# A two-block transformer on one Trainium2 core: attention matmuls moved to full-array float32r on stacked hi and lo parts

## The chip, the cores and the metric

The kernel runs on one core of a Trainium2 chip. The time is the device time of one execution in microseconds (us), and smaller is better. Before the change the median of three runs is 3154.35 us (3149.34 to 3155.27).

## What is computed

Two hybrid layers and two further layers (called even and odd here) act on 512 tokens of width 1024; all tensors are float32. Cut to the parts that matter, a hybrid layer is

```python
proj = rms_norm(x) @ w_in                      # nine pieces of 256 columns
ret  = bidirectional_retention(rq, rk, rv)     # 4 heads of 64, scores times a decay, no softmax
pool = multiscale_pool(pv)
na   = neighbourhood_attention(nq, nk, nv)     # 4 heads of 64, 256 keys for each block of 128 queries
mo   = memory_attention(mq, mk, mv)            # 4 heads of 64, 256 memory keys
x    = x + (sum of sigmoid(h @ w_gate) * (branch @ w_branch)) @ w_out
x    = x + ffn(x)                              # hidden width 2816
```

The even layer has sliding window attention (8 heads of 64, window 128) and latent attention (8 heads whose keys have 64 plain and 32 rotary channels, the rotary ones shared by all heads). The odd layer has 16 heads of 64 with a causal mask and dilated patterns. Each of the two is followed by cross attention (4 heads of 128) and an FFN.

## The kernel before

**Projections.** Activations lie feature-major, as 8 tiles of 128 channels by 512 tokens, each split into a part `hh` rounded to float32r and the rest `hl`. A weight chunk is loaded by SP (`ws`), rounded by ScalarE (`wh`, line 209) and its rest is taken by VectorE (`wl`, line 210). `mm3` (lines 217 to 219) then issues three float32r matmuls, hi·hi, lo·hi and hi·lo; `proj_tok` (lines 252 to 254) does the same with 256 moving columns. These are about 12,600 of the 15,023 TensorE instructions.

**Scores.** For two heads of 64, `stack_q` makes a tile for each head with the hi part of the query on one half of the partitions and the lo part on the other. `stack_k` gives the hi part of a head's key on both halves, and one tile `k[2]` with the lo parts of both heads. `scores` then needs two float32r matmuls, one of 128 rows (line 400) and one of 64 rows (line 401):

```python
nc.tensor.matmul(out=out, lhsT=q[b][:, qs], rhs=ks(k[b]), start=True, stop=False)
nc.tensor.matmul(out=out, lhsT=q[b][p, qs], rhs=ks(k[2])[p], start=False, stop=True)
```

Retention does the same with keys and queries exchanged (lines 714 and 715). The latent heads take one plain float32 matmul over 96 rows (line 1076).

**Weighted sums.** After the softmax (lines 425 to 440, mostly VectorE) the probabilities of a query block are transposed by TensorE (line 448), copied to SBUF as float32 (`PT`, line 451) and multiplied with the values in float32. The two heads go to the two halves of one PSUM tile `O`, each with 64 columns of the array: lines 471 (causal), 782 (neighbourhood), 494 (memory), 1029 (sliding window). Retention multiplies the scores with the decay on VectorE (line 717) and goes straight on (line 721, 512 moving columns).

**Order.** A scheduler fixes the order of each engine's instructions when the kernel is built. The code gives it the order of priority: `ORDER` for the hybrid layer (`R` retention, `N` neighbourhood, `M` memory, `B` the gated branches), and in `even` and `odd` the projection of the next heads ahead of the attention of these. `chunk` raises the priority of weight loading. Activations share one pool of 25 buffers (`act`, tag `a`); PSUM has two buffers each for `acc`, `S` (scores), `T` (transposes) and `O`.

Of the kernel before, what the change touches and what calls it, by code (L numbers as in the profile page):

```python
# [9 lines left out]
F32 = mybir.dt.float32  # L10
# [8 lines left out]
S = 512  # L19
# [79 lines left out]
class Net:  # L99
    def __init__(self, ctx, tc, a):  # L100
# [7 lines left out]
        self.pp = en(name="pp", bufs=4)  # L108
# [37 lines left out]
    def gains(self, *which):  # L146
        """Gain vectors as columns: rows of 128 are loaded and transposed on TensorE."""
# [31 lines left out]
    def split(self, src, scale=None, hi=None, lo=None):  # L179
        """hi/lo fp32r pair of src * scale."""  # L180
# [14 lines left out]
    def chunk(self, src, kt, n):  # L195
        """src: list of (dram ap [kt*128 rows, cols], column offset)."""
# [24 lines left out]
    def proj(self, hs, W, c0, ncols, evac, n=512, tags=("acc",)):  # L221
        """Feature-major W[:, c0:c0+ncols]^T @ h; evac(tile index, psum)."""
# [17 lines left out]
    def proj_tok(self, hs, ws, n, toks, evac, tags=("acc",)):  # L240
        """Token-major h^T W for chunks ws (list of (hi, lo, kt)); evac(token tile index, psum [128, n])."""
# [24 lines left out]
    def rsqrt(self, src, w, scale, out=None, last=False):  # L266
        """(src * scale + EPS) ** -0.5 for a small tile."""
# [16 lines left out]
    def norm_stats(self, acc, dim, name, want_bc=True):  # L284
        """acc: [128, 512] sums of squares over channel tiles -> token-major rstd [128, 4] and its broadcast."""
# [15 lines left out]
    def prep(self, k, g, start=False):  # L301
        """Split g * x for the next layer and add up its squares."""
# [45 lines left out]
    def feature_major(self, tiles, c):  # L348
        """Channels 128 c ... of token-major tiles [128, 2, *] -> PSUM [128, tokens]."""
# [10 lines left out]
    def stack_q(self, src, view=lambda t: t, gp=False):  # L360
        """Two heads of 64 on the partitions of src -> for each head a tile with its hi and its lo part."""
# [11 lines left out]
    def stack_k(self, src, g=None, gp=False, out=None):  # L373
        """Two heads of 64 on the partitions of src -> for each head its hi part twice, and the lo parts of both."""
        nc = self.nc
        out = out or [self.stack_tile(src.shape[-1], gp) for _ in range(3)]
# [9 lines left out]
        kl = out[2]  # L386
        for b in range(2):
            p = slice(64 * b, 64 * b + 64)
            if g is None:
                nc.vector.tensor_tensor(out=kl[p], in0=src[p], in1=out[b][p].bitcast(F32), op=OP.subtract)  # L390
            else:
                nc.vector.scalar_tensor_tensor(out=kl[p], in0=src[p], scalar=g[p], in1=out[b][p].bitcast(F32),
# [896 lines left out]
```

## Time and profile before

| what | value |
|---|---|
| median of three runs | 3154.35 us |
| profiled execution, span | 3152.4 us |
| TensorE busy | 3083.4 us, 98% |
| VectorE busy | 1689.0 us, 54% |
| ScalarE busy | 1254.3 us, 40% |
| GpSimd busy | 354.9 us, 11% |
| mean granted TensorE clock | 0.984 |

The page of the profile gives only the span of the profiled execution, which is 2 us under the median. Busy time of TensorE counts a matmul up to its modelled end, so neighbouring matmuls overlap: its real cost is the distance from one start to the next, which the timeline shows. DMA engines are busy 30% of the span.

### The profile page before, as it was taken

The numbers are of one execution on the slowest core, as the hardware profiler recorded it, in microseconds if no ns is written. First come the engines' busy times: TensorE is split into PE (matmuls) and PEld (weight loads), VectorE is DVE, ScalarE is ACT, GpSimd is POOL, SyncE is SP. The second block draws the span as 40 slices with busy tenths as digits, with TensorE's granted clock in tenths as the row PEclk, the third lists the DMA queues.
The fourth block names the chain that finished last, engine by engine and source line by source line (L and its number), as shares of the span: only waits on it lengthen the run. The fifth ranks groups of instructions, "written<-read, shape, count | busy, mean of one in ns | idle before, by whom it ended". The sixth has DMA issues, their size and how long they took to land.

```text
span 3152.4 us, 39048 instructions
## 1 busy us (share of the span) xinstructions
PE 3083.4 (98%) x15023; PEld 2500.8 (79%) x15023; DVE 1689.0 (54%) x3054; ACT 1254.3 (40%) x2126; POOL 354.9 (11%) x635
## 2 busy tenths in 40 slices
PE   7989999999999999999999999999999999999998
PEld 6767788888886778888888668788888777888887
DVE  6555555444565564664445775554446666554444
ACT  6443333222463433432223655432225666442222
POOL 2410121000132011120000101010000000010100
PEclk9989999999999999999999899999999999999999
DMA  5312242233342223332322213233332211333332
GB/s 160 108 46 87 73 134 94 96 98 95 126 126 63 70 84 94 124 98 94 100 91 82 52 38 98 74 100 101 94 97 92 66 57 57 94 92 96 100 95 80
DMA packets 288532, 285.62 MB, mean 91 GB/s; under 512 B 23637, under 2 KB 280026, under 8 KB 288346
## 3 DMA queue, kind: packets, MB, share of 16 engines
q1 hardware_dynamic: 288345, 283.13, 29.4%
q8 instruction: 118, 1.93, 0.3%
q14 instruction: 69, 0.56, 0.1%
HBM read 275.37 MB, written 7.71 MB: 90 GB/s over the span
## 4 chain that ended last, share of the span: by engine, by line
PE 95%; DVE 3%; ACT 1%; DMA 1%; issue 1%; POOL 0%; SPq 0%; DVEq 0%; ACTq 0%
PE p_acc L217 11%; PE p_acc L218 11%; PE p_acc L219 11%; PE p_O L217 7%; PE p_O L218 7%; PE p_O L219 7%; PE p_S L218 7%; PE p_S L217 7%; PE p_S L219 7%; PE p_acc L252 2%; PE p_acc L253 2%; PE p_acc L254 2%; PE p_T L448 2%; PE p_S L401 2%; PE p_O L471 1%; PE p_S L400 1%
## 5 line engine op out<-in xcount | busy, mean ns | idle before, releaser
L210 DVE TENSOR_TENSOR wl<-ws,wh 128x1024 fp32r<-128x1024 f32 (+1 forms) x512 | 613.4, 1198 | 751.7 <-ACT wh L209 750.6
L209 ACT CAST wh<-ws 128x1024 fp32r<-128x1024 f32 (+1 forms) x512 | 516.5, 1009 | 1120.2 <-issue 363.1
L217 PE MATMUL p_acc<-hh,wh 128*128 128x512 f32 x1000 | 394.6, 396 | 1.7 <-DVE x L829 1.7
L218 PE MATMUL p_acc<-hh,wl 128*128 128x512 f32 x1000 | 392.5, 393 | 0.0
L219 PE MATMUL p_acc<-hl,wh 128*128 128x512 f32 x1000 | 391.4, 393 | 0.0
L217 PE MATMUL p_O<-hh,wh 128*128 128x512 f32 x680 | 264.4, 390 | 0.3 <-DVE al L188 0.3
L218 PE MATMUL p_O<-hh,wl 128*128 128x512 f32 x680 | 264.5, 390 | 0.0
L219 PE MATMUL p_O<-hl,wh 128*128 128x512 f32 x680 | 264.4, 389 | 0.0
L218 PE MATMUL p_S<-hh,wl 128*128 128x512 f32 x624 | 244.1, 391 | 2.8 <-DVE wl L210 2.8
L217 PE MATMUL p_S<-hh,wh 128*128 128x512 f32 x624 | 243.7, 392 | 2.5 <-ACT wh L209 2.1
L219 PE MATMUL p_S<-hl,wh 128*128 128x512 f32 x624 | 243.7, 391 | 0.0
L571 POOL TENSOR_TENSOR fa<-fa,R_x 128x512 f32<-128x512 f32 x88 | 115.7, 1317 | 1092.6 <-DVE fa L570 1086.2
L217 PEld LDWEIGHTS p_acc<-hh,wh 128*128 128x128 f32 x1000 | 189.0, 189 | 43.9 <-DVE x L829 2.3
L219 PEld LDWEIGHTS p_acc<-hl,wh 128*128 128x128 f32 x1000 | 188.9, 189 | 40.5 <-issue 0.8
L218 PEld LDWEIGHTS p_acc<-hh,wl 128*128 128x128 f32 x1000 | 189.0, 189 | 39.2 <-issue 1.0
L217 PE MATMUL p_acc<-ah,wh 128*128 128x512 f32 x444 | 177.9, 402 | 1.7 <-DVE mlak L1051 1.7
L218 PE MATMUL p_acc<-ah,wl 128*128 128x512 f32 x444 | 174.0, 392 | 0.0
L219 PE MATMUL p_acc<-al,wh 128*128 128x512 f32 x444 | 172.7, 393 | 0.0
L217 PE MATMUL p_S<-ah,wh 128*128 128x512 f32 x392 | 153.3, 392 | 0.3 <-ACT ah L187 0.3
L218 PE MATMUL p_S<-ah,wl 128*128 128x512 f32 x392 | 153.1, 391 | 0.0
L219 PE MATMUL p_S<-al,wh 128*128 128x512 f32 x392 | 151.7, 389 | 0.0
L217 PEld LDWEIGHTS p_O<-hh,wh 128*128 128x128 f32 x680 | 127.5, 188 | 27.2 <-DVE al L188 0.7
(374 smaller groups left out, 5736.0 us busy)
## 6 DMA issues: line engine op xcount, KB each, us to landing
ws<-w_ffn_in SPq DMA_DIRECT2D x88, 512.0 KB
ws<-w_gate SPq DMA_DIRECT2D x64, 512.0 KB
ws<-l_w_gate SPq DMA_DIRECT2D x44, 512.0 KB
ws<-l_w_up SPq DMA_DIRECT2D x44, 512.0 KB
ws<-w_ffn_out SPq DMA_DIRECT2D x40, 512.0 KB
ws<-l_w_down SPq DMA_DIRECT2D x40, 512.0 KB
ws<-w_in SPq DMA_DIRECT2D x36, 512.0 KB
ws<-l_w_qkv SPq DMA_DIRECT2D x24, 512.0 KB
```

The source lines that it names most:

```text
L209: nc.scalar.copy(wh, st)
L210: nc.vector.tensor_tensor(out=wl, in0=st, in1=wh.bitcast(F32), op=OP.subtract)
L217: nc.tensor.matmul(out=out, lhsT=wh[part, k, cols], rhs=hh[part, hn], start=start, stop=False)
L218: nc.tensor.matmul(out=out, lhsT=wl[part, k, cols], rhs=hh[part, hn], start=False, stop=False)
L219: nc.tensor.matmul(out=out, lhsT=wh[part, k, cols], rhs=hl[part, hn], start=False, stop=stop)
L252: nc.tensor.matmul(out=o, lhsT=hh[:, t0:t0 + 128], rhs=wh[:, kk, :], start=k == 0, stop=False)
L253: nc.tensor.matmul(out=o, lhsT=hh[:, t0:t0 + 128], rhs=wl[:, kk, :], start=False, stop=False)
L254: nc.tensor.matmul(out=o, lhsT=hl[:, t0:t0 + 128], rhs=wh[:, kk, :], start=False, stop=k == K - 1)
L400: nc.tensor.matmul(out=out, lhsT=q[b][:, qs], rhs=ks(k[b]), start=True, stop=False)
L401: nc.tensor.matmul(out=out, lhsT=q[b][p, qs], rhs=ks(k[2])[p], start=False, stop=True)
L448: nc.tensor.transpose(pt[:, 128 * i:128 * i + 128], b, self.ident)
L571: nc.gpsimd.tensor_tensor(out=a, in0=a, in1=R, op=OP.mult)
```

## The change

All matmuls of retention, neighbourhood, memory, sliding window, latent and causal attention become float32r over the full 128 by 128 array.

- `stack_k` makes four tiles, the lo part of each head now on both halves as well, so that both matmuls of `scores` have 128 rows.
- Values are kept as `[hi | lo]` side by side, 128 columns (`stack_v`, a ScalarE and a VectorE operation). `transposes` leaves the transposed probabilities as a hi and a lo tile, and `weigh` issues two matmuls for each head.
- The result stands in one PSUM tile for each head, its two halves still to be added: `join` copies one half (ScalarE) and adds the other (VectorE).
- `attend_causal` handles two query blocks at a time, so most products have 256 moving columns; a block on the diagonal and all of neighbourhood attention have 128. Sliding window attention puts both heads side by side in the moving operand.
- A latent head takes three float32r matmuls, with the shared rotary key stacked once (`krot`).
- Neighbourhood attention loads its value tiles for each pair of heads (64 small DMAs in a layer where there were 32).
- `P` and `PT` move to the pool of the stage, with 4 or 5 and 5 or 6 buffers; cross attention keeps float32 (`split=False`).

```diff
     def stack_k(self, src, g=None, gp=False, out=None):
-        out = out or [self.stack_tile(src.shape[-1], gp) for _ in range(3)]
+        out = out or [self.stack_tile(src.shape[-1], gp) for _ in range(4)]
...
-        kl = out[2]
         for b in range(2):
             p = slice(64 * b, 64 * b + 64)
...
+            for d in (b, 1 - b):
+                kl = out[2 + b][64 * d:64 * d + 64]
+                if g is None:
+                    nc.vector.tensor_tensor(out=kl, in0=src[p], in1=out[b][p].bitcast(F32), op=OP.subtract)
...
     def scores(self, out, q, k, b, qs, ks):
         nc.tensor.matmul(out=out, lhsT=q[b][:, qs], rhs=ks(k[b]), start=True, stop=False)
-        nc.tensor.matmul(out=out, lhsT=q[b][p, qs], rhs=ks(k[2])[p], start=False, stop=True)
+        nc.tensor.matmul(out=out, lhsT=q[b][:, qs], rhs=ks(k[2 + b]), start=False, stop=True)
+
+    def stack_v(self, out, src, scale=None):
+        hi, lo = out[:, :, 0:64], out[:, :, 64:128]
+        if scale is None:
+            nc.scalar.copy(hi, src)
+            nc.vector.tensor_tensor(out=lo, in0=src, in1=hi.bitcast(F32), op=OP.subtract)
...
+    def weigh(self, out, v, pt, cols, start, stop):
+        nc.tensor.matmul(out=out, lhsT=v, rhs=pt[0][:, cols], start=start, stop=False)
+        nc.tensor.matmul(out=out, lhsT=v, rhs=pt[1][:, cols], start=False, stop=stop)
+
+    def join(self, o, O, b, scale=None):
+        p, q = slice(64 * b, 64 * b + 64), slice(64 - 64 * b, 128 - 64 * b)
...
+            nc.scalar.copy(tv, O[q])
+            nc.vector.tensor_tensor(out=o[p], in0=O[p], in1=tv, op=OP.add)
...
-    def attend_causal(self, heads, scale, bias, O):
...
+    def attend_causal(self, heads, scale, bias):
+        Os = [self.psum("O") for _ in heads]
+        for i0 in (0, 2):
...
+            for b, (_, vs) in enumerate(heads):
+                for js in ([(0, 1)] if i0 == 0 else [(0, 1), (2, 3)]):
+                    blocks = [(j, i) for j in js for i in (i0, i0 + 1) if j <= i]
+                    pt = self.transposes([Ps[b, i][:, 128 * j:128 * j + 128] for j, i in blocks])
...
+                        self.weigh(Os[b][:, 128 * first:128 * i0 + 256], vs(j), pt,
+                                   slice(128 * at[0], 128 * at[-1] + 128), j == 0, j == i0 + 1)
+        o = self.at(name="ao")
+        for b in range(2):
+            self.join(o, Os[b], b)
...
         def retention(hp):
-                    nc.tensor.matmul(out=Sp, lhsT=ks[2][p, kc], rhs=qs[b][p], start=False, stop=True)
-                    P = self.pp.tile([128, 512], F32, name="RP", tag="P")
+                    nc.tensor.matmul(out=Sp, lhsT=ks[2 + b][:, kc], rhs=qs[b], start=False, stop=True)
+                    P = self.pt_tile(F32)
                     nc.vector.tensor_tensor(out=P, in0=Sp, in1=Gs[b][:, 384 - 128 * i:896 - 128 * i], op=OP.mult)
-                    Ps.append(P)
+                    hi, lo = self.pt_tile(), self.pt_tile()
+                    self.split(P, None, hi, lo)
+                    Ps.append((hi, lo))
...
-                                         lhsT=nv[cb][:, ch, 64 * h:64 * h + 64],
-                                         rhs=pt[:, 256 * ch + 128 * b:256 * ch + 128 * b + 128], start=ch == 0, stop=ch == 1)
+                        self.weigh(Os[b][:, 128 * cb:128 * cb + 128], nv[cb][:, ch, 128 * b:128 * b + 128], pt,
+                                   slice(256 * ch + 128 * b, 256 * ch + 128 * b + 128), ch == 0, ch == 1)
```

The schedule changes with it. The first place is TensorE at the end of the first hybrid layer's retention, the second pair of heads, before:

```order
L721 MATMUL p_O_1630<-RP_1667,rv0_567 64x512
L714 MATMUL p_S_1676<-stack_1618,stack_1622 128x512
L715 MATMUL p_S_1676<-stack_1618,stack_1623 128x512
L721 MATMUL p_O_1630<-RP_1674,rv1_568 64x512
L714 MATMUL p_S_1683<-stack_1615,stack_1621 128x512
L715 MATMUL p_S_1683<-stack_1615,stack_1623 128x512
L721 MATMUL p_O_1630<-RP_1679,rv1_568 64x512
L714 MATMUL p_S_1688<-stack_1618,stack_1622 128x512
L715 MATMUL p_S_1688<-stack_1618,stack_1623 128x512
```

and with the change:

```order
L416 MATMUL p_O_1662<-PT_1715,rv1_567 128x512
L417 MATMUL p_O_1662<-PT_1716,rv1_567 128x512
L758 MATMUL p_S_1745<-stack_1643,stack_1649 128x512
L759 MATMUL p_S_1745<-stack_1643,stack_1651 128x512
L416 MATMUL p_O_1661<-PT_1728,rv2_568 128x512
L417 MATMUL p_O_1661<-PT_1729,rv2_568 128x512
L758 MATMUL p_S_1754<-stack_1646,stack_1650 128x512
L759 MATMUL p_S_1754<-stack_1646,stack_1652 128x512
```

Each weighted sum is now two matmuls over all 128 columns (lines 416 and 417), into a tile `p_O` of its own for each head, and stands between scores of 128 rows; as before, no projection stands there.

The second place is VectorE in the last causal attention of the odd layer (`c_dil` is the mask, `sm_m`, `sm_n`, `sm_l` and `sm_r` are softmax vectors of one column; the softmax lines are 425 to 440 before and 456 to 471 now), before:

```order
L440 TENSOR_SCALAR P_22246<-P_22246,sm_r_22253 128x256
L188 TENSOR_TENSOR al_22178<-p_O_21999,ah_22177 128x512
L425 ISA P_22314,sm_m_22315<-p_S_22311,c_dil_19777 128x512
L425 ISA sm_m_22315 128x1
L439 RECIPROCAL sm_r_22277<-sm_l_22272 128x1
L425 ISA P_22327,sm_m_22328<-p_S_22324,c_dil_19777 128x512
L425 ISA sm_m_22328 128x1
L439 RECIPROCAL sm_r_22290<-sm_l_22285 128x1
L428 TENSOR_SCALAR sm_n_22317<-sm_m_22315 128x1
L440 TENSOR_SCALAR P_22270<-P_22270,sm_r_22277 128x384
```

and with the change:

```order
L187 TENSOR_TENSOR PT_23212<-p_T_23207,PT_23211 128x384
L471 TENSOR_SCALAR P_23278<-P_23278,sm_r_23285 128x128
L470 RECIPROCAL sm_r_23298<-sm_l_23293 128x1
L471 TENSOR_SCALAR P_23291<-P_23291,sm_r_23298 128x128
L187 TENSOR_TENSOR PT_23225<-p_T_23219,PT_23224 128x512
L456 ISA P_23304,sm_m_23305<-p_S_23301,c_dil_20638 128x256
L456 ISA sm_m_23305 128x1
L456 ISA P_23317,sm_m_23318<-p_S_23314,c_dil_20638 128x256
L456 ISA sm_m_23318 128x1
L429 TENSOR_TENSOR ao_23244<-p_O_23064,join_23245 64x512
```

Subtractions of the lo part of the transposed probabilities (line 187) and the join of the halves (line 429) now stand in the queue between the softmax operations.

The third place is SP's queue in the first hybrid layer, where the neighbourhood values come back from DRAM (`nvd` to `nvt`), before:

```order
L665 DMA nvd_1309<-nvz 128x256 x2
L674 DMA nvt<-nvd_1309 32x256 x8
L665 DMA nvd_1309<-nvz 128x256
L674 DMA nvt<-nvd_1309 32x256 x5
L665 DMA nvd_1309<-nvz 128x256
L674 DMA nvt<-nvd_1309 32x256 x19
L202 DMA ws<-w_in 128x4x256
L202 DMA ws<-w_gate 128x4x256 x2
L758 DMA nab<-rpd 16x384 x3
```

and with the change:

```order
L706 DMA nvd_1320<-nvz 128x512 x3
L201 DMA ws<-w_in 128x4x256
L706 DMA nvd_1320<-nvz 128x512
L201 DMA ws<-w_gate 128x4x256 x2
L804 DMA nab<-rpd 16x384 x4
L201 DMA ws<-w_branch 128x2x256
L804 DMA nab<-rpd 16x384 x9
L717 DMA nvt<-nvd_1320 32x256 x32
L201 DMA ws<-w_gate 128x4x256
```

Before, all 32 loads stood ahead of the first gate chunk; now two gate chunks, a branch chunk and most of the bias rows (`nab`) stand ahead of them, and the next gate chunk waits behind all 32. The loads of the second pair of heads (not shown) come a few chunks later.

## Rows read from the trace of the kernel before

**Rows 1.** The page: the span, busy time of engines, the chain by engine.

```profile
span 3152.4 us, 39048 instructions
...
PE 3083.4 (98%) x15023; PEld 2500.8 (79%) x15023; DVE 1689.0 (54%) x3054; ACT 1254.3 (40%) x2126; POOL 354.9 (11%) x635
...
PE 95%; DVE 3%; ACT 1%; DMA 1%; issue 1%; POOL 0%; SPq 0%; DVEq 0%; ACTq 0%
```

**Rows 2.** Windows: from:to, length, busy PE PEld DVE ACT POOL, clock, DMA share, GB/s.

```profile
125.00:181.00 56.00, 49.32 (x225) 30.33 (x226) 25.37 (x45) 15.81 (x28) 12.11 (x48) 0.91 0.23 66
181.00:275.00 94.00, 91.24 (x502) 73.44 (x502) 53.28 (x144) 41.85 (x86) 3.93 (x19) 0.96 0.24 71
275.00:375.00 100.00, 100.00 (x484) 77.78 (x484) 55.16 (x109) 37.40 (x74) 15.06 (x10) 1.00 0.26 79
1750.00:1925.00 175.00, 166.09 (x856) 115.55 (x855) 124.26 (x441) 97.27 (x260) 16.20 (x43) 0.89 0.13 38
1850.00:1875.00 25.00, 22.99 (x132) 16.13 (x130) 21.04 (x70) 13.30 (x34) 0.00 (x0) 1.00 0.14 45
2425.00:2660.00 235.00, 232.24 (x1377) 179.33 (x1376) 150.71 (x435) 161.16 (x339) 0.00 (x0) 0.98 0.18 56
1789.00:1813.00 24.00, 20.61 (x75) 13.13 (x76) 18.28 (x67) 11.68 (x37) 1.52 (x2) 0.50 0.00 1
```

**Rows 3.** Timeline of TensorE in retention: start, duration (us), line, operation.

```profile
157.39 1.07 PE L721 MATMUL p_O<-RP,rv 128*64 128x512 f32 x2
158.39 0.51 PE L714 MATMUL p_S<-stack 128*128 128x512 f32 x1
158.82 0.49 PE L715 MATMUL p_S<-stack 64*128 64x512 f32 x1
159.25 1.07 PE L721 MATMUL p_O<-RP,rv 128*64 128x512 f32 x2
```

**Rows 4.** Timeline of TensorE in the odd layer's attention.

```profile
2606.32 0.44 PE L471 MATMUL p_O<-PT,dv 128*64 128x128 f32 x4
2606.69 0.39 PE L400 MATMUL p_S<-stack 128*128 128x256 f32 x1
2607.00 0.38 PE L401 MATMUL p_S<-stack 64*128 64x256 f32 x1
2607.31 0.66 PE L471 MATMUL p_O<-PT,dv 128*64 128x128 f32 x8
```

**Rows 5.** Timeline of TensorE in the odd layer: projections, the first behind a score.

```profile
2451.69 0.50 PE L217 MATMUL p_acc<-hh,wh 128*128 128x512 f32 x1
2452.03 0.40 PE L218 MATMUL p_acc<-hh,wl 128*128 128x512 f32 x1
2452.26 0.39 PE L219 MATMUL p_acc<-hl,wh 128*128 128x512 f32 x1
...
2465.74 0.28 PE L254 MATMUL p_acc<-wh,hl 128*128 128x256 f32 x1
2465.86 0.28 PE L252 MATMUL p_acc<-wh,hh 128*128 128x256 f32 x1
```

**Rows 6.** Groups by line and shape, TensorE: count, busy us, mean ns.

```profile
L494 PE MATMUL p_O<-PT,mv 128*64 128x128 f32 x128 | 10.1, 284 | 0.1
L782 PE MATMUL p_O<-PT,nvt 128*64 128x128 f32 x128 | 10.1, 284 | 0.0
```

**Rows 7.** Groups by line and shape, VectorE and ScalarE.

```profile
L390 DVE TENSOR_TENSOR stack<-dk,stack 64x512 fp32r<-64x512 f32 x16 | 10.9, 683 | 0.9 <-PE p_S L401 0.6
L188 DVE TENSOR_TENSOR al<-p_O,ah 128x512 fp32r<-128x512 f32 x28 | 19.2, 686 | 39.3 <-ACT ah L187 39.3
L717 DVE TENSOR_TENSOR RP<-p_S,G 128x512 f32<-128x512 f32 x32 | 22.0, 688 | 36.9 <-PE p_S L715 35.3 <-ACT G L703 1.6
L771 DVE TENSOR_TENSOR bm<-nab,small_cst 128x256 f32<-128x256 f32 x24 | 9.6, 418 | 13.9 <-DMA nab<-rpd 9.1 <-DMA sink<-l_sinks 4.8
L187 ACT CAST ah<-fa 128x512 fp32r<-128x512 f32 x88 | 54.5, 619 | 103.4 <-DVE fa L576 103.3
```

More of the change, by code (lines that the diff above doesn't have):

```diff
@@ L474, in attend_mem @@
-    def attend_mem(self, heads, scale, O):
-        nc = self.nc
-        nh = len(heads)
-        step = 3 - nh
-        dv = 128 // nh
-        for i0 in range(0, 4, step):
-            yield
-            Ps = {}
-            for i in range(i0, i0 + step):
-                for b, score, _ in heads:
-                    Sp = self.psum("S")
-                    score(Sp[:, :256], b, i)
-                    Ps[b, i] = self.softmax(Sp[:, :256], 256, scale)
-            w = 128 * step
-            pt = self.transposes([Ps[b, i][:, 128 * j:128 * j + 128] for j in range(2) for b in range(nh)
-                                  for i in range(i0, i0 + step)])
-            for j in range(2):
-                for b in range(nh):
-                    o = w * (nh * j + b)
-                    nc.tensor.matmul(out=O[dv * b:dv * b + dv, 128 * i0:128 * i0 + w], lhsT=heads[b][2](j), rhs=pt[:, o:o + w],
-                                     start=j == 0, stop=j == 1)
+        if not split:
+            s = self.pt_tile(F32)
+            nc.scalar.copy(s[:, :n], pt[:, :n])
+            return s
@@ new lines, in attend_mem @@
+    def attend_mem(self, heads, scale, done):
+        nc = self.nc
+        for b, (score, vs) in enumerate(heads):
+            O = self.psum("O")
+            for i0 in (0, 2):
+                yield
+                Ps = {}
+                for i in (i0, i0 + 1):
+                    Sp = self.psum("S")
+                    score(Sp[:, :256], i)
+                    Ps[i] = self.softmax(Sp[:, :256], 256, scale)
+                pt = self.transposes([Ps[i][:, 128 * j:128 * j + 128] for j in range(2) for i in (i0, i0 + 1)], len(heads) == 2)
+                for j in range(2):
+                    out, cols = O[:, 128 * i0:128 * i0 + 256], slice(256 * j, 256 * j + 256)
+                    if len(heads) == 2:
+                        self.weigh(out, vs(j), pt, cols, j == 0, j == 1)
+                    else:
+                        nc.tensor.matmul(out=out, lhsT=vs(j), rhs=pt[:, cols], start=j == 0, stop=j == 1)
+            done(b, O)
@@ L960, in even @@
         ks = []
-        vtok = self.at((128, 4, 128), name="swv")
+        vtok = [self.act.tile([128, 4, 128], F32R, name="swv", tag="a") for _ in range(2)]
         def ev_kv(j, ps):
@@ L1073, in mla_proj @@
-                nc.vector.tensor_tensor(out=u[64:96], in0=ps[96:128], in1=Sq[96:128], op=OP.mult)
-                nc.vector.tensor_tensor(out=q[64:96], in0=q[64:96], in1=u[64:96], op=OP.add)
-                def score(Sp, i, n, q=q, k=kh[b]):
-                    nc.tensor.matmul(out=Sp[:, :n], lhsT=q[0:96, 128 * i:128 * i + 128], rhs=k[0:96, :n], start=True, stop=True)
-                hs.append((score, (lambda b: lambda j: vv[:, j, 64 * b:64 * b + 64])(b)))
+                qc = self.act.tile([128, 512], F32R, name="mlaqc", tag="a")
```

291 lines of the change are left out of this document (164 added, 127 removed).

## The prediction, before the result was known

> **What bounds the kernel now.** I read the page first: TensorE is busy 98% of the span and holds 95% of the chain [rows 1]. So time taken from TensorE shows in the end, except where another engine then becomes the limit. That is asked stage by stage, in the windows [rows 2]. Memory attention of the first hybrid layer (275 to 375 us) has TensorE at 100 of 100 us and VectorE at 55. Neighbourhood (181 to 275) has 91 of 94 and VectorE at 53. Retention (125 to 181) has 49 of 56. The even layer's attention (1750 to 1925) has TensorE at 166 of 175 us, but VectorE already at 124, and the granted clock is 0.89. The odd layer's (2425 to 2660) has 232 and 151 of 235. The two hybrid layers are alike, so each of the first three counts twice. Last, the timeline gives what a matmul really costs, from one start to the next [rows 3 to 5].
>
> Prices from there. A projection of 512 moving columns takes .23 us, one of 256 takes .12 [rows 5]. A score pair with its 64-row half takes .31 + .31 at 256 columns [rows 4], .43 + .43 at 512 [rows 3], though two full-array matmuls would be .24 and .46. The first projection behind such a pair takes .34 in place of .23 [rows 5], so the switch costs .1 more. I take one score pair at 256 columns to fall by .31 + .31 − .24 + .10 = .48 us.
>
> **Memory attention.** 16 score pairs in a layer: 16 × .48 = 7.7 us less. Its weighted sums are busy 10.1 us in two layers [rows 6], 5.05 in one; they become 4 heads × 2 block pairs × 2 key blocks × hi and lo = 32 matmuls of 256 columns, 32 × .12 = 3.8, so 1.2 less. The added VectorE work (lo of the transposes, `join`) lies under TensorE, which is busy all through with VectorE at 55%. Sum −8.9 a layer.
>
> **Neighbourhood.** Scores again −7.7. The weighted sums, 5.05 [rows 6], become 64 float32r matmuls of 128 columns, which no row prices. Low end .06, half of the 256-column row; high end .21: the fp32 matmul of 512 columns takes about 1.0 in retention [rows 3], some four times a float32r one, and short ones might fall back to that. I take .12, the nearest row. 64 × .12 = 7.7, so +2.6 (−1.2 to +8.4), and the layer −5.1 (−8.9 to +0.7). SP now issues the 32 value loads of a pair behind gate chunks and bias rows, and the next gate chunk behind the loads. I price that at 0: two gate chunks and a branch chunk go ahead of them in the order, and DMA is busy .24 of this stretch [rows 2]. If that cover is gone, TensorE waits for the chunk, 2 to 3 us a layer.
>
> [...]
>
> **Retention.** One head and key block takes 1.86 us of TensorE now, from one L721 to the next (157.39 to 159.25) [rows 3]: the two heads' fp32 records stand between scores and do not overlap. It becomes four matmuls of 512 columns, .91, so −.95. In the order, projections stand between half of the 16 in a layer: 8 × .95 = 7.6 us less. Between the other 8 nothing stands (the first order listing). There the loop sets the pace: scores .45, L717 .69, rounding on ScalarE .62, the lo part .69 [rows 7], weighted sum .45, together 2.9 for two in flight (two score buffers), so 1.45 at best; VectorE alone is 1.38. With hand-overs I take 1.75 (1.45 to 2.1): 8 × .1 = .8 less (3.3 less to 1.9 more). The last `join` is exposed: one copy and one add, .62 + .69 = 1.3 more. Sum −7.1 a layer.
>
> Hybrid layers: 2 × (−8.9 − 5.1 − 7.1) = −42 us.
>
> **Even and odd: VectorE.** Both keep TensorE near full now, and the change loads VectorE. A subtract or add of 512 columns takes .69 (L390 on 64 partitions, L188 on 128), of 256 columns .42 [rows 7], of 384 about .55 between them. *Even*: lo parts of transposes 20 × .69 + 16 × .55 + 4 × .42 ≈ 24; `join` 16 × .42 + 8 × .69 ≈ 12; the fourth stack tile and its second subtract 11; query stacks and latent queries 5.5 + 5.5; values 3.4; less some 8 for latent tiles that fall away: about +54, so 124 → 178, more than the 175 us that the stage takes [rows 2]. *Odd*: lo parts 32 × .55 + 16 × .69 = 28.6, `join` 11, stacks 11, values 5: about +56, so 151 → 207. TensorE falls there from 232 by 64 pairs × .48 = 31 to 201, and by some 6 more as the weighted sums go from 80 × .37 (the step of L471 x4 in [rows 4]) to 64 × .24 + 64 × .12. So in both VectorE is the longer one.
>
> How full can VectorE run? Its queue is in order, and the lo subtract (waits for ScalarE's rounding) and the `join` add now stand between softmax operations (the second order listing): whatever waits there holds up the softmax of the next block. The only full row is the 25 us from 1850 where it reaches 21.0, or .84, with TensorE still the limit [rows 2]; the upper end is 1.0. I take .90, between them and nearer the row. 178/.9 = 198, +23; 207/.9 = 230, −5. Sum **+18** us.
>
> **Sum.** −42 + 18 = −24 against the profiled execution's span, 3152.4, gives 3128; the median stands 2 us above that span, so **3130 us**. ScalarE gains about 140 operations and stays under half; GpSimd, gates, FFNs and cross attention keep their work and are priced at nothing. Ends: VectorE at 1.0 (385 us for both stages, 25 less than now), cheap short matmuls (8 less) and retention at 1.45 (5 less): −42 − 25 − 13 = −80, 3074. VectorE at .84 (385/.84 − 410 = +48) with dear short matmuls (+12): +18, 3172.
>
> **Rivals.**
> *A: the scheduler fills VectorE.* At a share of 1.0 even takes 178 (+3) and odd 207 (−28), the sum −42 − 25 = −67, 3085 us. For it: softmax and projections of other heads are independent work, and even and odd put the next heads' projection ahead. Against: no stretch of before shows VectorE over .84. Chance .13.
>
> *B: VectorE's queue turns the gain into a loss.* At a share s the two stages take 385/s against 410 now, and the hybrid gain is 42, so it is slower once 385/s passes 452, at s = .85. That is just what the fullest row reached [rows 2]. At .83 the sum is +12, at .82 +17: 3166 to 3172 us. For it: the in-order queue, the waits between ScalarE and VectorE for each transpose, and only 25 `act` buffers, which latent projections now share with more stacks. Against: in that row VectorE wasn't the limit. Chance .21.
>
> *C: TensorE's clock.* [...] Chance .14.
>
> [...]
>
> **How the numbers follow.** The forecast has .52, A .13, C .14, B .21. A run can tell some 0.2% (6 us). Forecast and A are faster by more, .65; C is the same, .14; B slower, .21. The range leaves out the far half of A and the tail of B: 3082 to 3172; the forecast's own is 3100 to 3147 (VectorE at .97 to .87).
>
> **What would show it.** Right: score pairs at .24 with no .10 behind them; L416 and L417 at .12 for 256 and .23 for 512; the memory stage about 9 us shorter and still full; retention's uncovered steps near 1.75; even longer by some 20 us, odd about as now, both with VectorE over .88 and TensorE with idle put down to `PT`, `P` or `O`. Wrong, and how: 128-column L416 well above .12 (neighbourhood); even and odd both shorter (A); both longer with VectorE under .85 (B); granted clock under .9 in odd or under .85 in even (C). A long idle before a gate chunk would be SP's order, which I priced at nothing.

## The result and the profile after

The changed kernel is 1.4% slower: 3197.05 us median of four runs (3195.91 to 3199.93) against 3152.78 of the kernel before beside it, a ratio of 1.0143 (95% interval 1.0129 to 1.0157). The profiled execution has a span of 3193.8 us, 41.4 over that of [rows 1].

Its page, the lines that answer to [rows 1]:

```profile
span 3193.8 us, 39092 instructions
...
PE 3044.1 (95%) x14743; PEld 2540.4 (80%) x14743; DVE 1852.0 (58%) x3377; ACT 1331.7 (42%) x2265; POOL 353.4 (11%) x627
...
PE 84%; DVE 8%; ACT 3%; issue 1%; POOL 1%; DMA 1%; SPq 1%; DVEq 0%; ACTq 0%
```

TensorE's busy time fell by 39 us, and the span grew by 41: TensorE now waits. Its share of the chain went from 95% to 84%.

Where does it wait? All kernels here issue the same 12,600 projection matmuls, so the same-numbered one marks the same amount of projection work done. The table gives what lies between two such marks in the trace before, and how much longer or shorter the change is there. A stage's border moves a little where a scheduler shifts projections into or out of it, so the three stretches of a hybrid layer are best read as a sum.

| stretch | first hybrid layer, before | change | second, before | change |
|---|---|---|---|---|
| up to the end of retention | 176.6 | −3.3 | 101.9 | +0.3 |
| neighbourhood | 81.6 | +15.9 | 67.4 | +16.5 |
| memory and branches | 109.6 | −12.0 | 137.6 | −13.0 |
| layer | | **+0.6** | | **+3.8** |

The even layer is 26.5 us longer (attention 179.1 to 203.8, cross attention 1.8), the odd layer's attention 11.4 (255.5 to 266.8). FFNs are equal to 0.1 us. The same stretches as windows (columns as in [rows 2]), before and then after:

```profile
196.00:277.50 81.50, 78.74 (x399) 61.01 (x398) 45.44 (x112) 35.44 (x69) 0.15 (x2) 0.96 0.23 70
1756.50:1935.60 179.10, 170.19 (x870) 118.65 (x869) 126.26 (x443) 100.04 (x264) 19.02 (x47) 0.90 0.14 41
2408.40:2663.90 255.50, 252.74 (x1476) 196.52 (x1475) 160.70 (x452) 173.00 (x356) 4.64 (x14) 0.98 0.19 58
```

```profile
192.30:289.80 97.50, 85.05 (x435) 72.50 (x434) 60.33 (x154) 44.37 (x91) 0.00 (x0) 0.89 0.27 77
220.00:230.00 10.00, 7.27 (x32) 6.54 (x31) 9.90 (x45) 5.92 (x18) 0.00 (x0) 0.50 0.37 106
1760.70:1964.50 203.80, 167.29 (x774) 130.71 (x773) 172.21 (x537) 133.37 (x328) 13.88 (x32) 0.88 0.14 39
2439.10:2705.90 266.80, 239.22 (x1348) 203.38 (x1347) 207.61 (x545) 181.70 (x370) 3.23 (x12) 0.95 0.18 56
```

VectorE has 46 us more in even and 47 in odd, and is busy .845 and .78 of them, while TensorE falls from .95 to .82 and from .99 to .90. In neighbourhood attention VectorE is at .62, so it isn't short of time; TensorE still falls from .97 to .87. So the stages have to be read one by one.

**Neighbourhood.** TensorE's timeline in the first hybrid layer, at the second pair of heads:

```profile
212.28 0.27 PE L417 MATMUL p_O<-PT,nvt 128*128 128x128 f32 x1
214.70 0.39 PE L399 MATMUL p_S<-stack 128*128 128x256 f32 x1 [2.15 <-ACT stack L384]
...
237.78 0.30 PE L416 MATMUL p_O<-PT,nvt 128*128 128x128 f32 x1 [1.19 <-DMA nvt<-nvd]
...
240.18 0.80 PE L216 MATMUL p_acc<-ah,wh 128*128 128x512 f32 x1 [1.76 <-DVE gz L868]
```

Between 212.3 and 240.2 us no projection runs at all. Before, projections stood between these scores, transposes and sums, as in these two rows of that trace:

```profile
231.93 0.38 PE L401 MATMUL p_S<-stack 64*128 64x256 f32 x1
232.24 0.50 PE L217 MATMUL p_acc<-hh,wh 128*128 128x512 f32 x1
```

The wait for a value load (`nvt`) at 237.8 is one of two, 2.4 us together in this stage; the prediction priced SP's order at nothing. The next projection waits for `gz`, the eviction of a gate projection whose last matmul had begun at 210.9. VectorE's timeline shows when that came:

```profile
238.85 0.68 DVE L429 TENSOR_TENSOR nao<-p_O,join 64x512 f32<-64x512 f32 x1 [5.19 <-ACT join L428]
239.46 1.27 DVE L868 TENSOR_TENSOR gz<-p_acc,R_x 128x512 f32<-128x512 f32 x2
```

The two evictions stand behind the join of the pair, 28 us after their input was there, though VectorE idled 5.2 us just ahead of it. Both buffers of `p_acc` were held all that time. That VectorE takes its queue in order is seen where the order is known: in the odd layer it ran the ten operations of the second order listing as they are listed, from 2665.38 us on, with 1.31 us idle ahead of the second L187 (2667.84) and the next softmax behind it (2668.45). So what has to be found is why the scheduler put the evictions there.

**Retention.** TensorE's cycle for a head and key block with no projection in it, to be held against [rows 3]:

```profile
152.02 0.50 PE L758 MATMUL p_S<-stack 128*128 128x512 f32 x1
152.35 0.40 PE L759 MATMUL p_S<-stack 128*128 128x512 f32 x1
152.73 0.50 PE L416 MATMUL p_O<-PT,rv 128*128 128x512 f32 x1
153.45 0.49 PE L417 MATMUL p_O<-PT,rv 128*128 128x512 f32 x1 [0.22 <-DVE PT L187]
154.05 0.50 PE L758 MATMUL p_S<-stack 128*128 128x512 f32 x1
```

It takes 2.03 us, 1.86 before: the four matmuls are short, and TensorE waits .22 us for VectorE's lo part.

**Even.** VectorE's timeline when the first latent heads are prepared, beside sliding window attention:

```profile
1800.11 0.67 DVE L1106 TENSOR_TENSOR mlak<-p_acc,R_ckv 128x512 f32<-128x512 f32 x1
1800.71 0.68 DVE L1113 TENSOR_TENSOR mlavT<-p_acc,R_ckv 128x512 f32<-128x512 f32 x1
...
1801.87 2.79 DVE L390 TENSOR_TENSOR stack<-mlak,stack 64x512 fp32r<-64x512 f32 x4
...
1806.85 2.12 DVE L368 TENSOR_TENSOR stack<-swq,stack 64x512 fp32r<-64x512 f32 x3
...
1810.78 0.33 DVE L456 CUSTOM_DVE_ANT_0 P<-p_S,c_swa,sink 128x128 f32<-128x128 f32 x1
```

For 10.7 us VectorE prepares operands (with one join and one split between), and no softmax starts. What it waits for itself, over the whole stage (total us, times, longest):

```profile
DVE ao L429 <- ACT join L428: 6.7, 3, 5.3
DVE PT L187 <- ACT PT L186: 6.0, 6, 2.3
DVE P L456 <- PE p_T L482: 4.9, 7, 1.7
```

The first two are hand-overs of this change: the join, and the lo part behind ScalarE's rounding. The third, a softmax that waits until a transpose has released a `P` tile, isn't new: VectorE waited longer for it in this stage before.

```profile
DVE P L425 <- PE p_T L448: 16.4, 18, 2.2
```

### The profile page after: what moved, and what is told of

It is laid out like the page before. It is cut to its first block, busy times and chain, and to the rows that moved or that the text cites. A ratio compares the mean times of both kernels' runs of the same rounds, so it can differ in the third digit from the quotient of the medians.

```text
span 3193.8 us, 39092 instructions
## 1 busy us (share of the span) xinstructions
PE 3044.1 (95%) x14743; PEld 2540.4 (80%) x14743; DVE 1852.0 (58%) x3377; ACT 1331.7 (42%) x2265; POOL 353.4 (11%) x627
## 4 chain that ended last, share of the span: by engine, by line
PE 84%; DVE 8%; ACT 3%; issue 1%; POOL 1%; DMA 1%; SPq 1%; DVEq 0%; ACTq 0%
PE p_acc L216 10%; PE p_acc L217 10%; PE p_acc L218 10%; PE p_O L216 7%; PE p_O L217 7%; PE p_O L218 7%; PE p_S L216 7%; PE p_S L217 7%; PE p_S L218 7%; PE p_acc L251 2%; PE p_acc L252 2%; PE p_acc L253 2%; DVE wl L209 1%; PE p_T L482 1%; SPq L717 1%
## 5 line engine op out<-in xcount | busy, mean ns | idle before, releaser
L216 PE MATMUL p_acc<-hh,wh 128*128 128x512 f32 (+1 forms) x1000 | 391.0, 392 | 1.2 <-DVE dv L411 1.2
L217 PE MATMUL p_acc<-hh,wl 128*128 128x512 f32 (+1 forms) x1000 | 391.6, 392 | 0.0
L218 PE MATMUL p_acc<-hl,wh 128*128 128x512 f32 (+1 forms) x1000 | 390.7, 392 | 0.0
L216 PEld LDWEIGHTS p_acc<-hh,wh 128*128 128x128 f32 (+1 forms) x1000 | 188.2, 188 | 40.5 <-DVE dv L411 1.4
L218 PEld LDWEIGHTS p_acc<-hl,wh 128*128 128x128 f32 (+1 forms) x1000 | 188.1, 188 | 39.4
L217 PEld LDWEIGHTS p_acc<-hh,wl 128*128 128x128 f32 (+1 forms) x1000 | 188.2, 188 | 38.4
L218 PEld LDWEIGHTS p_O<-hl,wh 128*128 128x128 f32 x680 | 127.7, 188 | 26.5
```

Of the source, the lines that this page charges most:

```text
L216: nc.tensor.matmul(out=out, lhsT=wh[part, k, cols], rhs=hh[part, hn], start=start, stop=False)
L217: nc.tensor.matmul(out=out, lhsT=wl[part, k, cols], rhs=hh[part, hn], start=False, stop=False)
L218: nc.tensor.matmul(out=out, lhsT=wh[part, k, cols], rhs=hl[part, hn], start=False, stop=stop)
```

## The experiments

The kernel before ran beside each of them (medians 3151.0 to 3153.3 us). The table gives each run's ratio and how its layers stand to the profiled execution before, by the same marks; "even" has its cross attention.

| run | us | ratio, interval | first hybrid | second | even | odd |
|---|---|---|---|---|---|---|
| the change | 3197.1 | 1.0143 (1.0129 to 1.0157) | +0.6 | +3.8 | +26.5 | +11.4 |
| e1 joins in another pool | 3188.2 | 1.0115 (1.0099 to 1.0132) | −8.1 | −3.3 | +26.2 | +18.4 |
| e2 scores alone | 3116.2 | 0.9888 (0.9873 to 0.9902) | −14.7 | −13.1 | −4.9 | −7.3 |
| e3 sums alone | 3245.0 | 1.0293 (1.0278 to 1.0308) | +9.4 | +14.1 | +47.8 | +19.0 |
| e4 no lo of probabilities | 3173.4 | 1.0064 (1.0049 to 1.0079) | 0.0 | −1.0 | +12.6 | +6.5 |
| e5 latent scores fp32 | 3195.0 | 1.0132 (1.0115 to 1.0149) | +1.0 | +3.7 | +12.7 | +19.8 |
| e6 head by head | 3182.7 | 1.0093 (1.0078 to 1.0108) | +1.6 | +4.8 | +20.9 | +1.8 |
| e7 half of that | 3192.6 | 1.0123 (1.0108 to 1.0138) | +0.9 | +4.5 | +24.6 | +11.0 |
| e8 no join add | 3175.8 | 1.0071 (1.0056 to 1.0086) | −5.4 | −1.7 | +17.7 | +8.9 |
| e9 e1 (hybrid) and e6 | 3167.9 | 1.0045 (1.0030 to 1.0060) | −6.3 | −1.9 | +20.9 | +2.2 |
| e10 key lo on GpSimd | 3197.6 | 1.0140 (1.0123 to 1.0157) | +2.9 | +3.3 | +25.6 | +11.6 |
| e11 e2 and GpSimd | 3107.5 | 0.9852 (0.9838 to 0.9867) | −17.6 | −11.2 | −11.7 | −10.8 |
| e12 no lo of keys | 3171.0 | 1.0062 (1.0045 to 1.0080) | −6.3 | −2.9 | +26.3 | +2.1 |
| e13 e2 and latent scores | 3119.9 | 0.9905 (0.9890 to 0.9919) | −12.4 | −12.8 | −1.5 | −6.4 |
| e14 e9, latent fp32 | 3158.0 | 1.0022 (1.0013 to 1.0032) | −8.9 | −1.9 | +9.1 | +2.9 |

One caution ahead of all: e5 changes nothing in the odd layer, and yet that layer is 8.4 us longer than in the change, since the scheduler ordered the whole program anew (the same instructions stand there in another order). e11 against e2 shows the same for even. Its edit is in `stack_k`, which e2 doesn't call in that layer, and both have the same instructions there; yet the attention takes 167.5 us in place of 174.2, at the same VectorE work (the granted clock is .97 and .91). The windows, e2 and then e11 (columns as in [rows 2]; a few instructions fall on the other side of their edges):

```profile
1728.80:1903.00 174.20, 160.89 (x869) 115.56 (x868) 125.63 (x443) 99.22 (x264) 19.06 (x47) 0.91 0.14 42
1715.80:1883.30 167.50, 152.35 (x875) 110.64 (x874) 125.56 (x447) 97.33 (x261) 16.21 (x48) 0.97 0.15 43
```

A difference of up to 8 us in odd or 7 in even is therefore put down to nothing unless several runs repeat it. Besides, each row of the table is one profiled execution, and the executions of one kernel lie 1.5 to 9.5 us apart.

### e1: the joins' tiles from another pool

```diff
-        t = self.t(name="join")
+        t = self.at(name="join")
...
-            o = self.t(name="nao")
+            o = self.at(name="nao")
```

> The changed kernel with the tiles join and nao taken from the pool of activations (act) in place of the pool of five temporaries (tmp), which the gates' evictions also use. Nothing else differs. Theory 1, the loss in neighbourhood attention (the traces show it 16 us longer in each hybrid layer, with no projection between the second pair's matmuls) comes from the temporaries: gates of the next branch can't be evicted until the joins have had their tiles, so TensorE has nothing to fill in with. Then projections come back between the second pair's matmuls and the two layers get back 25 to 40 us: 3155 to 3170; more if the same holds between a projection and an attention in the even and odd layers. Theory 2, the loss is VectorE's added work and in-order queue: the time stays within 8 us of the change's 3197. Theory 3, the late value loads and the gate chunk behind them in SP's queue: also within 8 us of 3197.

Neighbourhood attention stands at +0.7 and +1.5 in place of +15.9 and +16.5. VectorE's timeline there:

```profile
208.11 0.69 DVE L868 TENSOR_TENSOR gz<-p_acc,R_x 128x512 f32<-128x512 f32 x1 [1.69 <-PE p_acc L218]
212.79 0.69 DVE L868 TENSOR_TENSOR gz<-p_acc,R_x 128x512 f32<-128x512 f32 x1
216.92 0.68 DVE L429 TENSOR_TENSOR nao<-p_O,join 64x512 f32<-64x512 f32 x1
218.76 0.69 DVE L429 TENSOR_TENSOR nao<-p_O,join 64x512 f32<-64x512 f32 x1
```

Two gate evictions now come ahead of the join and not 28 us late behind it, and projections stand between the scores again. The value loads and SP's order are what they were, so theory 3 is out as the cause of the 16 us (and the waits for `nvt` are gone), and theory 2 as well; e9 and e14 repeat the result (+1.1 to +1.9). The size was less than expected: the layers got 8.7 and 7.1 back, 16 together and not 25 to 40, because memory attention's −12 became −6 (part of what neighbourhood lost had only moved across the border). The even layer doesn't answer at all. Odd is 7 worse, within the caution above.

### e2 and e3: either half alone

In the kernel before, for e2:

```diff
-        out = out or [self.stack_tile(src.shape[-1], gp) for _ in range(3)]
+        out = out or [self.stack_tile(src.shape[-1], gp) for _ in range(4)]
...
-        nc.tensor.matmul(out=out, lhsT=q[b][p, qs], rhs=ks(k[2])[p], start=False, stop=True)
+        nc.tensor.matmul(out=out, lhsT=q[b][:, qs], rhs=ks(k[2 + b]), start=False, stop=True)
```

For e3 the same lines in reverse, in the changed kernel.

> The kernel before with the full-array scores alone (four stack tiles, both matmuls of 128 rows, in retention too); weighted sums and latent scores stay as before. If a score pair is .48 us cheaper wherever TensorE bounds: hybrid 2 x 32 pairs of 256 and 2 x 16 of 512 (about .4 each) give 2 x (15.4 + 6) = 43 less, odd 64 pairs 31 less, even 32 pairs up to 15 less, against 11 + 4 us of VectorE work in odd and even: about 3153 - 43 - 31 - 5 = 3074. If the fourth stack tile and VectorE's second subtract cost as much as they bring: 3120 to 3150.

> The changed kernel with the 64-row second score matmul put back (three stack tiles), latent heads too; weighted sums, transposes in two parts and joins as in the change. If the weighted sums are what makes the change slower, this is slower still than the change: the scores' gain is lost as well where TensorE bounds, 3197 + 15 to 40 = 3210 to 3240. If the four stack tiles (pool of activations, VectorE) were the trouble, it is faster than the change: under 3190.

The scores alone are 1.1% faster than the kernel before, the sums alone 2.9% slower, each in every layer. The two differences, −36.8 and +92.1, add to +55, the change is +44. By layers the halves add up in odd (−7.3 and +19.0, the change +11.4) but not in even (−4.9 and +47.8, the change +26.5). The scores' gain is half of the 79 us that I expected, and the sums' loss 5 us beyond the range. A score pair in memory attention with the projection behind it, in the trace before and then in e2:

```profile
311.57 0.38 PE L401 MATMUL p_S<-mk,stack 64*128 64x256 f32 x1
311.88 0.50 PE L217 MATMUL p_acc<-hh,wh 128*128 128x512 f32 x1
312.21 0.39 PE L218 MATMUL p_acc<-hh,wl 128*128 128x512 f32 x1
```

```profile
299.97 0.66 PE L495 MATMUL p_O<-PT,mv 128*64 128x128 f32 x8
300.56 0.39 PE L401 MATMUL p_S<-mk,stack 128*128 128x256 f32 x1
300.78 0.28 PE L402 MATMUL p_S<-mk,stack 128*128 128x256 f32 x1
300.90 0.39 PE L217 MATMUL p_acc<-hh,wh 128*128 128x512 f32 x1
301.13 0.40 PE L218 MATMUL p_acc<-hh,wl 128*128 128x512 f32 x1
```

In e2 it is .34 us from the first score to what follows, not .24: the first score behind fp32 sums still takes .22. Over the 16 pairs of this stage the mean pair went from .60 (start to start, before) to .29, so .31 less each. The projection right behind a pair went from .34 to .23, but only 11 of the 16 pairs have one. So a pair is worth .31 + .10 × 11/16 = .38. Odd gained 7 where 64 × .31 = 20 was to be had.

### e4 and e8: VectorE's new work taken away

In e4:

```diff
-        hi, lo = self.pt_tile(), self.pt_tile()
-        self.split(pt[:, :n], None, hi[:, :n], lo[:, :n])
-        return hi, lo
+        hi = self.pt_tile()
+        nc.scalar.copy(hi[:, :n], pt[:, :n])
+        return hi, hi
```

In e8:

```diff
-            nc.scalar.copy(tv, O[q])
-            nc.vector.tensor_tensor(out=o[p], in0=O[p], in1=tv, op=OP.add)
+            nc.scalar.copy(o[p], O[p])
```

> The changed kernel without the lo part of the transposed probabilities after a softmax (the hi part is multiplied twice in its place, so TensorE does the same number of matmuls): it leaves out 120 VectorE subtractions and the wait on them; retention keeps its own. If VectorE's added work is what lengthens the even and odd layers (26 and 12 us by the traces), some 24 and 29 us of VectorE work fall away and both layers come back to at or under the time of before: 3197 - 40 to - 60 = 3137 to 3157. If it is the temporaries handed to the joins, as in theory 1 of the first run, the time falls by less than 20 us: over 3177.

> The changed kernel without the join's addition on VectorE (ScalarE copies one half of each result straight to its place; the other half is left out; retention keeps its join). It takes 12 and 11 us of VectorE work out of the even and odd layers and 2 joins of .7 us out of each pair of heads elsewhere. VectorE's work as the limit: even and odd shorter by about 10 us each, 3177. The in-order queue or the hand-over at a join worth more than its time: below 3170. Joins of no matter: over 3190. In neighbourhood attention the temporaries are handed out as in the change, so I expect no change of it there beyond 3 us.

e4 gave 23.6 us, 14 of them in even, where 18 us of VectorE work fell away (172.2 to 154.4 busy). It fell between its two readings: VectorE's work matters, and a half of the even layer's loss stays without the lo parts. e8 gave 21.3 us, 9 of them in even for 11.5 us of VectorE work. Its last sentence was a miss: neighbourhood attention got 5 and 9 us back, so a join that doesn't use its temporary, or asks less of VectorE, frees the gates too; this run doesn't say which.

### e5: latent scores as before

```diff
-            kh = self.stack_k(kt, gp=True)
+            kh = []
+            for b in range(2):
+                t = self.gp.tile([128, 512], F32, name="mlak", tag="gate")
+                nc.vector.tensor_tensor(out=t[0:64], in0=ps[64 * b:64 * b + 64], in1=R3[64 * b:64 * b + 64], op=OP.mult)
...
+                    nc.tensor.matmul(out=Sp[:, :n], lhsT=q[0:96, 128 * i:128 * i + 128], rhs=k[0:96, :n], start=True, stop=True)
```

> The changed kernel with latent heads' scores as before (one fp32 matmul over 96 rows, no stacks of query and key); weighted sums stay as in the change. Theory 1, VectorE's work sets the even layer's end: some 17 to 20 us of it fall away, so the even layer is 15 to 20 us shorter than the change's (it is 26 us over the time before): 3177 to 3182. Theory 2, the loss is in the weighted sums and joins, or in where tiles are handed out: within 6 us of 3197, or longer, since TensorE's fp32 scores come back.

(The rotary table's cosine isn't set to one on the rows of the plain channels here, which the kernel before does once with one instruction; the number and kind of operations of the stage are those intended.) By its whole time, 3195.0, the run falls on theory 2's side. By layers it doesn't: even came down by 13.8 us for 12.6 us less of VectorE work, near theory 1, though TensorE took its fp32 scores back, and odd, untouched, came out 8.4 longer.

### e6 and e7: loops of causal attention exchanged

In e6:

```diff
-        Os = [self.psum("O") for _ in heads]
-        for i0 in (0, 2):
-            Ps = {}
+        for b, (score, vs) in enumerate(heads):
+            O = self.psum("O")
+            for i0 in (0, 2):
+                Ps = {}
```

(e7 keeps both O tiles and exchanges only the two inner loops, so that two P tiles are in use at a time.)

> The changed kernel with the loops of causal attention exchanged: one head after the other, so that one O tile and two P tiles are in use at a time in place of two and four; same instructions. If the two O tiles of a pair (of two in all) and the four P tiles (of four) keep the next block's softmax and weighted sums from starting, the odd layer falls from +11 to 0 or less and the even layer's latent part gets a little back: 3175 to 3187. If VectorE's work or its in-order queue is the limit: within 5 us of 3197.

> As the last, but only the four P tiles: within each pair of query blocks one head's softmaxes, transposes and sums come before the other's, both O tiles stay in use. If P tiles are what holds, it comes out as the exchanged loops do (3175 to 3187); if the O tiles, within 5 us of 3197 while the exchanged loops gain.

With the same instructions, odd fell from +11.4 to +1.8 and even by 5.6. e9 and e14 have the same loops and stand at +2.2 and +2.9 in odd, against +11.0 to +19.8 in the change, e1, e5, e7 and e10, whose odd layers have the change's work and both O tiles, so this difference holds in spite of the caution. e7 gave nothing there: P tiles alone don't hold. What is left is that the change takes two of two O tiles for a pair of heads, where before a pair shared one, so that the next pair's sums have to stand behind its joins. That this is the reason is argued, not shown: e6 also takes all of one head's blocks ahead of the other's, which e7 does only within two query blocks, no run gave `O` a third buffer, and of TensorE's waits in the change's odd layer only one, 1.1 us before a projection at its end, is put down to a join. Its longest sum of waits there is for the next pair's stacks, and e6 has none of these (total us, times, longest):

```profile
PE p_S L399 <- ACT stack L382: 7.5, 4, 3.1
```

### e9: the two repairs together

```diff
-        t = self.t(name="join")
+        t = self.at(name="join") if self.pw == 256 else self.t(name="join")
```

(and the loops of e6; `pw` is 256 in hybrid layers alone.)

> The changed kernel with two repairs together: in the hybrid layers alone the joins' tiles come from the pool of activations (the first run gave 15 us back there and lost 7 in the odd layer), and causal attention goes head by head (that gave back 10 us in odd and 5 in even). If the two causes are separate, the gains add: 3197 - 15 - 14 = 3168, hybrid layers under the time before by about 11, odd level with it, even still some 19 over it. If they share a cause (one VectorE queue), less: 3175 to 3185.

3167.9, the sum of the two. Even stays at +20.9.

### e10 to e12: VectorE's work on keys

In e10, and the same in e2's kernel for e11:

```diff
-                if g is None:
+                if d != b:
+                    nc.gpsimd.tensor_copy(kl, out[2 + b][p])
+                elif g is None:
```

In e12, in place of all of `stack_k`'s subtractions:

```diff
+        for b in range(2):
+            nc.gpsimd.memset(out[2 + b].bitcast(F32), 0.0)
```

> The changed kernel with the second copy of each key's lo part made by GpSimd from the first, in place of VectorE's second subtraction; same results. It takes 16 x .69 = 11 us of VectorE work out of odd and of even (6 of them in even's latent heads). If the even layer's length is VectorE's work over a share of .84, it falls by about 8 to 13 us and the odd one by 5 to 14: 3175 to 3187. If GpSimd's copy is late or slows VectorE, 3197 or more.

> The full-array scores alone, as in the second run (3116), with the second lo copy on GpSimd as in the last. There TensorE is busy .96 of the odd layer's attention and VectorE .68, so taking VectorE work away should bring little: 3108 to 3117. If VectorE's queue still held the scores back there (odd gained 7 where 64 x .3 = 19 was to be had), 8 to 12 us: 3104 to 3108.

> The changed kernel without the lo parts of the keys: the tiles stay, GpSimd sets them to zero, and the second score matmul multiplies these. It leaves out all of VectorE's subtractions for keys (16 x 4 x .69 us over the program's causal and latent heads: 22 us of VectorE work in odd, 11 in even, and some in the hybrid layers), and a score no longer waits for one. The previous run moved half of that work to GpSimd and gained nothing. If GpSimd's slower copy (.77 us, behind VectorE's) ate the gain: odd falls by 15 to 28 us and even by 10 to 13 here, 3150 to 3170. If work ahead of the scores is off the chain that sets the end, and only what stands between softmax and weighted sum counts: 3185 to 3197.

In the change, moving the copies gained nothing (GpSimd's copy is the slower one, .77 us against .69, and stands behind VectorE's subtraction; that this ate the gain isn't shown). The kernel with scores alone and the same edit is the fastest of this study, 3107.5, 8.7 us below e2. But 6.8 us of that are in even, where the edit changes no instruction (see the caution), and only 3.5 in odd, where the forecast looked for them: its second reading was met by luck, and what the copies on GpSimd bring is not shown. Leaving the keys' lo out altogether gave 26 us, to just over the first range: 7 in each hybrid layer and 9 in odd, but even didn't move, though VectorE's work there fell by 11 us. The windows of even (columns as in [rows 2]), e12 and then e14:

```profile
1747.60:1951.10 203.50, 168.93 (x773) 134.04 (x772) 160.78 (x521) 133.39 (x328) 16.99 (x40) 0.86 0.14 39
```

```profile
1746.10:1932.50 186.40, 161.14 (x741) 122.31 (x740) 159.64 (x517) 107.90 (x288) 17.80 (x39) 0.91 0.14 42
```

The same VectorE work, 160 us, takes 203.5 in the one and 186.4 in the other. So the even layer isn't simply VectorE's work divided by a share. These two kernels differ in ScalarE's work as well (133 and 108 us) and in the loops; e2 and e11 above show it with the same instructions on every engine, where only the order differs.

### e13 and e14: the latent part, alone and out of the repaired change

e13 is e2 with the change's latent projection and scores, e14 is e9 with the latent part of the kernel before (table set to one included); the edit in e14 is that of e5, in e13 its reverse.

> The full-array scores alone, as in the second run (3116, even layer 4.9 us under the time before), plus the latent heads' scores as three float32r matmuls with their stacks; weighted sums stay fp32. If preparing the latent heads costs what taking it out of the change gave back (14 us), even is 5 to 12 us over the time before: 3125 to 3133. If it costs only together with the weighted sums' VectorE work (a queue that overflows), even is within 4 us of the second run: 3112 to 3120.

> The repaired change (3168) with the latent heads' scores in fp32 as before. If the three causes are separate, the 14 us of the latent heads come off as well: 3154, level with the kernel before, even some 6 us over it. If the exchanged loops and the latent heads give back the same waits, 3160 to 3168.

Alone, the latent part costs even 3.4 us, with VectorE 135.7 busy of 177.6, or .76. Out of the repaired change it gives 11.8 back, with VectorE at .86 in both. So it seems to cost in full only where the sums have filled VectorE's queue; but the two differ by 8.4 us, little more than order alone did in even, so this isn't shown. e14 ends at 3158, between its two readings and 0.2% over the kernel before. e2, with the same latent scores and the new score pairs but without the new sums, is at 3116: with everything repaired that was found, the new sums still cost 42 us.

## Why the prediction was wrong, point by point

I forecast −24 us and got +41. Of the 65 us, 46 are the hybrid layers (−42 forecast, +4.4 measured), 16 the odd layer (−5 and +11.4), 3.5 the even layer (+23 and +26.5). Of the 46, e1 gives 16 back, so these are the pool of the joins' tiles, for which the sum had no term. The other 31 are terms of the wrong size: about 15 the score pairs, 12 retention, the rest not assigned.

- **Score pairs, a term mis-sized.** I priced one at .48 by taking both matmuls down to .12 and adding .10 for what follows. e2 shows .38 in memory attention: the first score behind other work keeps .17 of its .29 in the mean, so the pair itself falls by .31, and the .10 behind it is right but comes to 11 of 16 pairs. The 32 pairs of a hybrid layer were 15.4 us in the forecast, neighbourhood and memory of e2 together gained 7.9 and 8.1.
- **Memory attention**, −8.9: −6.3 and −5.0 in e1, where the stage stands by itself. The step, and that VectorE lies under TensorE there, were right; the size was the score price. The sums gained .4 (4.5 us start to start before, 4.1 in e1), where I had 1.2 from their busy time. Busy time is a poor price, since short records overlap; the full-array matmuls of the changed kernel do so as well (.28 us long, .11 apart). The distance is the better one: 32 fp32 matmuls of 128 columns in 4.5 us are .14 each, where a quarter of retention's 1.0 for 512 columns would be .25. Why they cost so little is not shown.
- **Neighbourhood**, −5.1, and +15.9 and +16.5 measured: this step failed. I looked for a wait in SP's queue and gave VectorE's join no term, since VectorE has time. The join's cost is not its .7 us. Its tiles come from the five temporaries that the gates' evictions need as well, the scheduler gave them out in such an order that the evictions came behind the joins, and with `p_acc` held TensorE lost its filler; e1 moved the tiles and got it back. The price of a 128-column matmul, on the other hand, was near (the 64 take 6.5 us from start to start in e1, 7.7 forecast).
- **Retention**, −7.1 a layer: −3.3 and +0.3. The uncovered cycle is 2.03 us, near the upper end of the 1.45 to 2.1 that I gave and over the 1.75 that I took; in e2 it is 1.66. (The two records between the scores in [rows 3] are one head's matmul and not two heads': the 32 matmuls of line 721 in the two layers left 64 records. The sum uses their time and isn't touched by it.) With scores alone (e2) the stretch is −6.8 and −5.0, so the sums gave back 3.5 and 5.3 of it.
- **Even.** The mechanism was right in the main, VectorE nearly full and TensorE waiting, and the size near. The share is .845, just under the .85 at which rival B began to decide, and not .90; my +54 of VectorE work was +46, which made up for a part. But the step "work over a share" is too simple, as e2 against e11 shows.
- **Odd.** The step that failed is VectorE as the one limit, at .90: it stands at .78, below either bound I gave it, with TensorE at .90, so neither engine was full. That VectorE's 207 us came true is luck: the window of [rows 2] leaves out 20 us of the stage (its work was 161 us, not 151), and the change added 47, not 56. I gave no term to how many tiles a pair of heads holds, or to the order of its blocks. e6 shows what these cost together, 9.6 us with the same instructions; which of the two it is stays open. Behind it VectorE stands at .81.
- **Rivals.** B came true in its sign and, for both stages, in its share, but its 3166 to 3172 rested on a hybrid gain of 42 that wasn't there. A fell. C fell: the granted clock is .88 in even and .95 in odd, above the marks set for it, and no run shows what lowers it. Neighbourhood attention, where I didn't look for it, fell to .89, and its stretch of 220 to 230 us is at 0.50. There TensorE lacked work first: it was busy 4.4 of the 10 us before, at a granted 0.80. What the clock adds to the 16 us isn't separated; in e1 the stage stands at +0.7 and its stretch (193.6 to 275.9) at 0.94.

What stays open: the even layer's 26 us come apart in too many ways (lo parts 14, latent stacks 14, joins 9, loops 6), which add to more than the whole. They share VectorE's queue, so they may cost by each other; the loops' 6 are repeated by e9, but lie within what order alone did. Why the keys' lo parts cost nothing in even (e12) I can only argue: they may stand where VectorE would otherwise have waited for ScalarE's join or rounding.

## What to carry to other kernels

When a change adds a small step to an evacuation, ask what the step's tiles are taken from and who else draws on that pool: a temporary that is held can stop an engine that never touches it, as TensorE here (e1 got 16 us back). Count PSUM tiles for each unit of work before and after; a change that doubles them can take away a double buffer (argued here, not shown, for e6's 9.6 us). Split a change that has two halves: here one was worth 1.1%, and the other cost more than that. And look for a stage that an edit doesn't touch: how far it moves is what a new order alone does, here up to 8 us.

## What the runs showed of the hardware that was not expected

A float32r matmul of 128 moving columns takes about as long as one of 256 when it stands behind another of 128, but half of that behind a projection of 512. TensorE's timeline of the changed kernel, and then of e1:

```profile
204.73 0.27 PE L416 MATMUL p_O<-PT,nvt 128*128 128x128 f32 x1
204.84 0.28 PE L417 MATMUL p_O<-PT,nvt 128*128 128x128 f32 x1
204.95 0.45 PE L218 MATMUL p_acc<-hl,wh 128*128 128x512 f32 x1
```

```profile
203.55 0.22 PE L416 MATMUL p_O<-PT,nvt 128*128 128x128 f32 x1
203.61 0.28 PE L417 MATMUL p_O<-PT,nvt 128*128 128x128 f32 x1
203.72 0.27 PE L416 MATMUL p_O<-PT,nvt 128*128 128x128 f32 x1
```

.11 us each from start to start in the first, against .12 for 256 columns and .23 for 512 [rows 5]. In e1 the one at 203.55 follows a projection and takes .06, as do all 21 of e1 that stand between a projection and another such matmul; the next takes .11. So of my two bounds, .06 and .21, the low one holds there; the .21 was my estimate, where a quarter of the 1.0 in [rows 3] would be .25, and neither is in these listings. What sets the .11 is not shown.
